# Earlier adding of bank halves in four FFNs, and another order of the first pairs in a fifth

## The chip, the core and the metric

The program runs on one core of one Trainium2 chip. The time is device microseconds of one execution; the kernel before took 1358.48 us (median of three runs, 1358.3 to 1360.25). The engines are named as in the profile: PE (TensorE, matmuls), PEld (its weight loads), DVE (VectorE), ACT (ScalarE), POOL (GpSimd) and SP, whose queue issues the weight transfers.

## What is computed

256 tokens of width 1024 pass through a first block of two layers and a second block of one. In every layer of the first block stands a pair of gated FFNs around a mixer; the second block ends in one FFN with a short convolution. Everything is float32.

```python
# block 1, twice: FFN, mixer, FFN
h = rms_norm(x, ffn1_norm[layer])
x = x + 0.5 * (silu(h @ w_gate) * (h @ w_up)) @ w_down      # 1024 -> 2816 -> 1024
h = rms_norm(x, mix_norm[layer]);  x = x + mixer(h)          # even_mixer, then odd_mixer
h = rms_norm(x, ffn2_norm[layer]); x = x + 0.5 * swiglu(h)   # a second FFN
# block 2
x = layer_norm(x); x = layer_norm(ALPHA * x + mixer2(x) @ w_o)
h = causal_conv3(x @ w_up)                                   # 1024 -> 2 * 2816
a, u = split(h);   x = layer_norm(ALPHA * x + (gelu(a) * u) @ w_down)
```

## The kernel before

Activations lie transposed: the 1024 features are 8 tiles of 128 partitions, each with 256 tokens in its free dimension. All weights stand in one stream of blocks of 128x1024 floats, in the order of their use. SP loads a block into `raw` (5 buffers), ACT casts it to float32r as `wh` (line 314), DVE takes the rest, `wl = raw - wh` (line 316); each of these has 5 buffers, so up to five blocks are ready ahead of PE. A product of one weight tile with the 8 input tiles (`proj_t`) uses one block and leaves its result in one PSUM bank.

In the FFNs of block 1 the moving operand is both parts of the input side by side, `xh | xl`, 512 columns (`mm2`, lines 334, 335 and 337). So a bank holds two halves of 256 tokens that still have to be added: `fold` (lines 597 to 600) copies the right half with ACT and adds the left one with DVE. The bank is free after that. Six banks take turns (`six_ps`: four named mm, two named sc); the others, aux, serve small products.

The function `ffn` (lines 549 to 595) goes over 22 tiles of the hidden layer. Each is a pair of products, gate and up. For a pair it issues both products, adds the gate's halves into `s`, multiplies by `rb` (the token factor of the norm, 1/rms of each token on all partitions), takes Silu with ACT into `sg`, adds the up product's halves into `hp`, multiplies, and splits the result into its high and low part `h`. `rb` comes from `norm_bcast` (lines 528 to 540): a product with ones for the sum of squares (line 532), three ACT steps and three DVE steps. In the first FFN the squares themselves are taken by ACT in between (`norm_sum_first`).

Block 2 starts its projections before its layer norm is known: the first six products are made of the raw input (`def_proj`, line 1090) and corrected afterwards on DVE (`def_out`, lines 1108 and 1110) into tiles `dv`. This happens ahead of its mixer (`mix2`) and again ahead of its FFN. Between them `ln_apply` makes the normed input tiles `xs` (lines 1059 to 1063).

The function `ffn2` (line 1463) goes over 22 pairs as well. The first six results, three pairs, are those `dv` tiles; from pair 3 on it issues the products. Each result gets its convolution: one ACT step (line 1478) and two DVE steps that add the shifted tokens (1479 and 1481), which for a product also free its bank. ACT takes Gelu (1484), POOL multiplies (1486), ACT and DVE split (1487 and 1488).

Tiles of 256 columns come from one set of 14 buffers (`tmp`, tag c1), those of 512 from one of 7 (c2). The tile framework's planner sets the order on each engine: it goes by the order in which the code is written and by when its own plan has an instruction ready. On the chip each engine then runs its list in order.

```python
s = self.tmp("s", T)
self.fold(s, pg)
nc.vector.tensor_tensor(out=s, in0=s, in1=self.rb, op=ALU.mult)
```

Of the kernel before, what the change touches and what calls it, by code (L numbers as in the profile page):

```python
# [9 lines left out]
F32 = mybir.dt.float32  # L10
F32R = mybir.dt.float32r
AF = mybir.ActivationFunctionType
ALU = mybir.AluOpType
AX = mybir.AxisListType

P = 128
T = 256
# [3 lines left out]
KF = DFF // P  # L21
BLK = 1024
NSLOT = 22
LOOK = 6
NWB = 5
NRAW = 5
NC1 = 14
NC2 = 7
WARM = 18
NDEF = 6  # L30
# [181 lines left out]
class K:  # L212
# [21 lines left out]
    def tmp(self, tag, n, bufs=2, dt=F32):  # L234
        if n == T:
            return self.tp.tile([P, T], dt, tag="c1", name=tag, bufs=NC1)
        if n == 2 * T:
# [290 lines left out]
    def norm_bcast(self):  # L528

        nc = self.nc  # L530
        ps = self.aux_ps()[:, :T]
        nc.tensor.matmul(ps, self.ones, self.acc, start=True, stop=True)
        u, y, t = [self.tmp(f"nb{i}", T) for i in range(3)]
        nc.scalar.activation(u, ps, AF.Identity, scale=1.0 / D, bias=self.eps[:, 0:1])
        nc.scalar.activation(y, u, AF.Ln)
        nc.scalar.activation(y, y, AF.Exp, scale=-0.5)
        nc.vector.scalar_tensor_tensor(out=t, in0=y, scalar=-0.5, in1=y, op0=ALU.mult, op1=ALU.mult)
        nc.vector.tensor_tensor(out=t, in0=t, in1=u, op=ALU.mult)
        self.rb = self.tmp("rb", T)
        nc.vector.scalar_tensor_tensor(out=self.rb, in0=t, scalar=1.5, in1=y, op0=ALU.add, op1=ALU.mult)  # L540

    def ln_exp_tables(self):
# [5 lines left out]
    def ffn(self, next_gain, first=False):  # L548
        nc = self.nc
        h2 = [self.slot(f"h{i}", F32R) for i in range(KF // 2)]  # L550
        if not first:
            self.norm_bcast()
        for i in range(KF):
            pg = self.six_ps()
            if i == 0 and first:
                self.look = 2
                self.proj_t(pg)
                self.norm_sum_first()
                self.norm_bcast()
                self.look = LOOK  # L560
            else:
                self.proj_t(pg)
            pu = self.six_ps()
            self.proj_t(pu)
            s = self.tmp("s", T)
            self.fold(s, pg)
            nc.vector.tensor_tensor(out=s, in0=s, in1=self.rb, op=ALU.mult)
            sg = self.tmp("sg", T)
            self.last_act = nc.scalar.activation(sg, s, AF.Silu)
            hp = self.tmp("hp", T)  # L570
            self.fold(hp, pu)
            nc.vector.tensor_tensor(out=hp, in0=hp, in1=sg, op=ALU.mult)
            nc.scalar.activation(self.hi(h2, i), hp, AF.Copy)
            nc.vector.tensor_tensor(out=self.lo(h2, i), in0=hp, in1=self.hi(h2, i).bitcast(F32), op=ALU.subtract)
        self.ln_exp_tables()
        if next_gain is not None:
            self.norm_begin()
        n = 0
        for j in range(KD):
            ps = self.mm_ps()  # L580
            for k in range(KF):
                if n % 8 == 0:
                    wh, wl = self.block()
                s = slice((n % 8) * P, (n % 8 + 1) * P)
                n += 1
                self.mm2(ps, wh[:, s], wl[:, s], self.both(h2, k), k == 0, k == KF - 1)
            t = self.tmp("t", T)
            self.fold(t, ps)
            nc.vector.scalar_tensor_tensor(out=t, in0=t, scalar=0.5, in1=self.rb,
                                           op0=ALU.mult, op1=ALU.mult)  # L590
            nc.vector.tensor_tensor(out=self.x(j), in0=self.x(j), in1=t, op=ALU.add)  # L591
            if next_gain is not None:
                self.norm_tile(j, next_gain)
            else:
                self.trans_tile(j)
# [504 lines left out]
    def def_out(self, i):  # L1100

        nc = self.nc
        ps = self.dps.pop(i)
        wb = self.tmp("wgb", 2, 4)
        nc.vector.tensor_copy(wb, ps[:, 256:258])
        v = self.tmp("dv", T)
        r = self.mA[nc.vector]
        nc.vector.scalar_tensor_tensor(out=v, in0=self.mA[nc.gpsimd][:, :T], scalar=wb[:, 0:1], in1=ps[:, :T],
                                       op0=ALU.mult, op1=ALU.subtract)
        nc.vector.tensor_tensor(out=v, in0=v, in1=r[:, T:], op=ALU.mult)  # L1110
        return v, wb[:, 1:2]
# [351 lines left out]
    def ffn2(self, first):  # L1463
        nc = self.nc
        h2 = [self.slot(f"h{i}", F32R) for i in range(KF // 2)]
        x2 = [self.slot(f"x2n{i}") for i in range(2)]
        for i in range(KF):
            y = []
            for u in range(2):
                c = u * KF + i  # L1470
                t = self.tmp("s" if u == 0 else "sg", T)
                if 2 * i + u < len(first):
                    ps, b = first[2 * i + u]
                    nc.scalar.activation(ps, ps, AF.Identity, bias=b)
                else:
                    ps = self.six_ps()[:, :T]
                    self.proj_t(ps)
                nc.scalar.activation(t, ps, AF.Identity, scale=self.col("conv2", c), bias=self.col("convb", c))
                nc.vector.scalar_tensor_tensor(out=t[:, 1:], in0=ps[:, :T - 1], scalar=self.col("conv1", c),
                                               in1=t[:, 1:], op0=ALU.mult, op1=ALU.add)  # L1480
                nc.vector.scalar_tensor_tensor(out=t[:, 2:], in0=ps[:, :T - 2], scalar=self.col("conv0", c),  # L1481
                                               in1=t[:, 2:], op0=ALU.mult, op1=ALU.add)
                y.append(t)
            self.last_act = nc.scalar.activation(y[0], y[0], AF.Gelu)
            hp = self.tmp("hp", T)
            nc.gpsimd.tensor_tensor(out=hp, in0=y[0], in1=y[1], op=ALU.mult)
            nc.scalar.activation(self.hi(h2, i), hp, AF.Copy)
            nc.vector.tensor_tensor(out=self.lo(h2, i), in0=hp, in1=self.hi(h2, i).bitcast(F32), op=ALU.subtract)
            if 8 <= i < 16:
                j = i - 8  # L1490
                ps = self.aux_ps()
                for tt in range(2):
                    nc.tensor.transpose(ps[:, tt * P:(tt + 1) * P], self.x(j)[:, tt * P:(tt + 1) * P], self.ident)
                    nc.scalar.activation(x2[tt][:, j * P:(j + 1) * P], ps[:, tt * P:(tt + 1) * P], AF.Copy,
                                         scale=2.0 ** 0.25)
        self.ln_exp_tables()
        gb = [self.slot(n) for n in ("lng", "lnb")]
        for t, n in zip(gb, ("f2g", "f2b")):
            nc.gpsimd.dma_start(out=t, in_=self.aps[n].to_broadcast([P, D]))
        st = self.tmp("bst", 36, 1).rearrange("p (t h s) -> p t h s", t=2, h=3)  # L1500
        n = 0
        for gi, (c0, cw) in enumerate(((0, 512), (512, 256), (768, 256))):
            ps = [self.mm_ps()[:, :cw] for _ in range(2)]
            held = []
            for k in range(KF):
                o = n % BLK
                if o == 0:
                    wh, wl = self.block()
                n += cw
                w = wh[:, o:o + cw], wl[:, o:o + cw]  # L1510
                late = gi == 2 and k >= KF - 16
                if late:
                    held.append((k, w))
                for tt in range(1 if late else 2):
                    self.down(ps[tt], h2, k, tt, w)
            for tt in range(2):
                if tt:
                    for k, w in held:
                        self.down(ps[1], h2, k, 1, w)
                x = x2[tt][:, c0:c0 + cw]  # L1520
                nc.vector.tensor_tensor(out=x, in0=ps[tt], in1=x, op=ALU.add)
                nc.vector.bn_stats(out=st[:, tt, gi], in_=x)
                if gi == 2:
                    self.ffn2_out(tt, x2[tt], st[:, tt], gb)
# [112 lines left out]
```

## Time and profile before

| | |
|---|---|
| median of 3 runs | 1358.48 us (1358.3 to 1360.25) |
| profiled execution, its own time | 1355.37 us |
| its span, first to last instruction | 1353.6 us |
| PE / PEld busy | 1315.9 us (97%) / 1165.5 us (86%) |
| DVE / ACT / POOL busy | 996.2 us (74%) / 812.5 us (60%) / 218.9 us (16%) |
| weight transfers | 231.49 MB, 48.5% of 16 DMA engines |
| mean granted TensorE clock | 0.997 |

The page's busy times are sums over stages; where PE stops is read from the waits and the timeline. In a timeline row stand the start and the duration in us, the engine, the line, the operation, the tiles written and read, and in brackets the idle time of the engine ahead of it with what ended it. The end of a matmul is modelled and overlaps the next one, so the pace of PE is read from start to start.

### The profile page before, as it was taken

What the parts mean: (1) busy time and instruction counts of PE and PEld (TensorE: products, weight loads), DVE (VectorE), ACT (ScalarE), POOL (GpSimd) and SP (SyncE); (2) the same over time, 40 slices, a digit from 0 to 9 for tenths busy, and PEclk for the clock granted to TensorE, in tenths of its full rate; (3) what the DMA queues carried; (4) which work ended last, traced back from release to release, by engine and by line L of the source; (5) the groups of instructions that cost most, each with busy time, mean ns of one, the idle gap of its engine ahead of it and who ended that gap; (6) DMA issues with size and microseconds to landing.
All of it is one profiled execution on the core that took longest, in us unless ns stands there. A gap on an engine that the chain in (4) does not pass through costs nothing.

```text
span 1353.6 us, 22502 instructions
## 1 busy us (share of the span) xinstructions
PE 1315.9 (97%) x8250; PEld 1165.5 (86%) x8250; DVE 996.2 (74%) x1860; ACT 812.5 (60%) x1491; POOL 218.9 (16%) x260
## 2 busy tenths in 40 slices
PE   8999999899999999999999999999999999889997
PEld 7888887798888888888899888888877888889987
DVE  7877677668776768776658777777877768887754
ACT  7655545756555446555468746555577556866642
POOL 2000141021000210001334340000134022321101
PEclk9999999999999999999999999999999999999999
DMA  8555565025555555555565345555555304355561
GB/s 291 187 187 188 188 203 185 1 98 198 187 188 187 189 184 188 187 187 186 187 233 187 126 145 190 190 190 187 187 187 179 117 32 156 119 193 174 196 208 46
DMA packets 64367, 231.49 MB, mean 171 GB/s; under 512 B 7352, under 2 KB 7488, under 8 KB 64256
## 3 DMA queue, kind: packets, MB, share of 16 engines
q1 hardware_dynamic: 61632, 221.41, 48.5%
q0 software_dynamic: 2480, 8.63, 1.8%
q8 instruction: 65, 1.06, 0.3%
q14 instruction: 46, 0.38, 0.1%
q10 hardware_dynamic: 144, 0.00, 0.0%
HBM read 228.96 MB, written 1.06 MB: 170 GB/s over the span
## 4 chain that ended last, share of the span: by engine, by line
PE 88%; DVE 5%; ACT 4%; issue 2%; DMA 0%; POOL 0%; SPq 0%; DVEq 0%; ACTq 0%
PE mm L337 25%; PE mm L335 14%; PE sc L337 7%; PE mm L341 5%; PE mm L342 5%; PE mm L343 5%; PE sc L335 4%; PE mm L372 4%; PE mm L370 4%; PE mm L371 4%; PE mm L334 3%; DVE wl L316 1%; PE sc L334 1%; PE mm L664 1%; ACT wh L314 1%
## 5 line engine op out<-in xcount | busy, mean ns | idle before, releaser
L316 DVE TENSOR_TENSOR wl<-raw,wh 128x1024 fp32r<-128x1024 f32 x409 | 507.0, 1242 | 250.3 <-ACT wh L314 249.0
L314 ACT ACTIVATE wh<-raw 128x1024 fp32r<-128x1024 f32 x417 | 440.2, 1059 | 416.1 <-issue 200.5
L337 PE MATMUL mm<-xs,wh 128*128 128x512 f32 x826 | 294.5, 396 | 0.0
L335 PE MATMUL mm<-xs,wl 128*128 128x256 f32 x944 | 244.1, 279 | 1.8 <-DVE wl L299 1.0
L337 PE MATMUL mm<-h,wh 128*128 128x512 f32 x672 | 237.9, 398 | 0.0
L335 PE MATMUL mm<-h,wl 128*128 128x256 f32 x704 | 191.5, 280 | 0.0
L335 PEld LDWEIGHTS mm<-xs,wl 128*128 128x128 f32 x944 | 177.7, 188 | 12.8 <-DVE wl L299 1.6
L337 PEld LDWEIGHTS mm<-xs,wh 128*128 128x128 f32 x826 | 154.6, 188 | 31.7 <-DVE xs L444 0.3
L337 PEld LDWEIGHTS mm<-h,wh 128*128 128x128 f32 x672 | 126.0, 188 | 29.2
L337 PE MATMUL sc<-xs,wh 128*128 128x512 f32 x406 | 144.8, 396 | 0.0
L335 PEld LDWEIGHTS mm<-h,wl 128*128 128x128 f32 x704 | 132.9, 189 | 3.1
L470 POOL TENSOR_TENSOR sq<-xt 128x256 f32<-128x256 f32 x40 | 34.8, 872 | 547.1 <-DVE xt L591 342.5
L335 PE MATMUL sc<-xs,wl 128*128 128x256 f32 x464 | 120.2, 280 | 0.0
L341 PE MATMUL mm<-xs,wh 128*128 128x256 f32 x384 | 109.9, 289 | 5.3 <-DVE s L1481 4.7
L342 PE MATMUL mm<-xs,wh 128*128 128x256 f32 x384 | 109.5, 286 | 1.1 <-DVE xs L1063 1.1
L343 PE MATMUL mm<-xs,wl 128*128 128x256 f32 x384 | 109.3, 286 | 0.0
L335 PEld LDWEIGHTS sc<-xs,wl 128*128 128x128 f32 x464 | 87.5, 189 | 5.1
L337 PEld LDWEIGHTS sc<-xs,wh 128*128 128x128 f32 x406 | 76.1, 188 | 15.5
L341 PEld LDWEIGHTS mm<-xs,wh 128*128 128x128 f32 x384 | 73.7, 193 | 7.4 <-issue 6.4
L342 PEld LDWEIGHTS mm<-xs,wh 128*128 128x128 f32 x384 | 74.2, 193 | 1.5 <-DVE xs L1063 1.3
L343 PEld LDWEIGHTS mm<-xs,wl 128*128 128x128 f32 x384 | 74.1, 193 | 0.9 <-issue 0.8
L372 PE MATMUL mm<-wh,xs 128*128 128x512 f32 x144 | 56.1, 394 | 1.2 <-DVE xs L1063 1.2
(392 smaller groups left out, 2573.8 us busy)
## 6 DMA issues: line engine op xcount, KB each, us to landing
raw<-wst SPq DMA_DIRECT2D x417, 512.0 KB, 3.3
m1b<-m1bias POOLq DMA_DIRECT2D x8, 512.0 KB, 5.1
xt<-xT SPq DMA_DIRECT2D x4, 256.0 KB, 5.0
patf<-m2pat POOLq DMA_DIRECT2D x2, 512.0 KB, 7.9
kb<-scr POOLq DMA_DIRECT2D x2, 512.0 KB, 3.9
out<-x2n SPq DMA_DIRECT2D x4, 256.0 KB, 2.0
raw<-wst SPq DMA_DIRECT2D x2, 256.0 KB, 4.6
m0tab<-m0tab POOLq DMA_DIRECT2D x1, 512.0 KB, 5.2
```

The lines of the kernel that those rows point to most:

```text
L314: self.nc.scalar.activation(wh[:, c], r[:, c], AF.Copy)
L316: e.tensor_tensor(out=wl[:, c], in0=r[:, c], in1=wh[:, c].bitcast(F32), op=ALU.subtract)
L334: mm(ps, wh, x2, start=True, stop=False)
L335: mm(ps[:, :T], wl, x2[:, :T], start=False, stop=False, skip_group_check=True)
L337: mm(ps, wh, x2, start=False, stop=last)
L341: mm(ps, wh, xh, start=first, stop=False)
L342: mm(ps, wh, xl, start=False, stop=False)
L343: mm(ps, wl, xh, start=False, stop=last)
L370: mm(ps, xh, wh, start=first, stop=False)
L371: mm(ps, xh, wl, start=False, stop=False)
L372: mm(ps, xl, wh, start=False, stop=last)
L470: nc.gpsimd.tensor_tensor(out=sq, in0=self.x(j), in1=self.x(j), op=ALU.mult)
```

## The change

Three things are edited. In `ffn` each product's halves are added right behind that product, ahead of the token factor, Silu writes over `s`, and in the first FFN the squares and the norm come after the first add. The token factor and its helpers get tiles of their own (nb with 3 buffers, rb with 2), c1 shrinks to 11, and `dv` tiles are taken as halves of 512-column tiles of c2. In `ffn2` the pairs are worked in the order 3, 4, 0, 5, 6, 1, 7, 8, 2, and then 9 to 21: the three pairs that come from `dv` stand later.

```diff
-NC1 = 14
+NC1 = 11
@@ norm_bcast
-        u, y, t = [self.tmp(f"nb{i}", T) for i in range(3)]
+        u, y, t = [self.tp.tile([P, T], F32, tag="nb", name=f"nb{i}", bufs=3) for i in range(3)]
...
-        self.rb = self.tmp("rb", T)
+        self.rb = self.tp.tile([P, T], F32, tag="rb", name="rb", bufs=2)
@@ ffn
-            pg = self.six_ps()
-            if i == 0 and first:
-                self.look = 2
-                self.proj_t(pg)
-                self.norm_sum_first()
-                self.norm_bcast()
-                self.look = LOOK
-            else:
-                self.proj_t(pg)
-            pu = self.six_ps()
-            self.proj_t(pu)
-            s = self.tmp("s", T)
-            self.fold(s, pg)
+            y = []
+            for u in range(2):
+                ps = self.six_ps()
+                if i + u == 0 and first:
+                    self.look = 2
+                self.proj_t(ps)
+                t = self.tmp("s" if u == 0 else "hp", T)
+                self.fold(t, ps)
+                if i + u == 0 and first:
+                    self.norm_sum_first()
+                    self.norm_bcast()
+                    self.look = LOOK
+                y.append(t)
+            s, hp = y
             nc.vector.tensor_tensor(out=s, in0=s, in1=self.rb, op=ALU.mult)
-            sg = self.tmp("sg", T)
-            self.last_act = nc.scalar.activation(sg, s, AF.Silu)
-            hp = self.tmp("hp", T)
-            self.fold(hp, pu)
-            nc.vector.tensor_tensor(out=hp, in0=hp, in1=sg, op=ALU.mult)
+            self.last_act = nc.scalar.activation(s, s, AF.Silu)
+            nc.vector.tensor_tensor(out=hp, in0=hp, in1=s, op=ALU.mult)
@@ def_out
-        v = self.tmp("dv", T)
+        if i % 2 == 0:
+            self.dv = self.tmp("dv", 2 * T)
+        v = self.dv[:, i % 2 * T:(i % 2 + 1) * T]
@@ ffn2
-        for i in range(KF):
+        for i in (3, 4, 0, 5, 6, 1, 7, 8, 2, *range(9, KF)):
```

How the lists change is seen at two places. The numbers of lines behind the edit are smaller by two in the changed kernel up to `def_out` (600 becomes 598, 1063 becomes 1061) and the same again in `ffn2`.

DVE at the start of the first FFN, before: L537, 538 and 540 make the token factor, L600 is the add of two halves, L567 the product with the factor.

```order
L1123 TENSOR_SCALAR g_9973<-g_9973 128x8
L316 TENSOR_TENSOR wl<-raw,wh 128x1024 x3
L537 SCALAR_TENSOR_TENSOR nb_221<-nb_220 128x256
L715 TENSOR_SCALAR nsink<-m0row 128x8
L538 TENSOR_TENSOR nb_221<-nb_221,nb_219 128x256
L316 TENSOR_TENSOR wl<-raw,wh 128x1024
L540 SCALAR_TENSOR_TENSOR rb<-nb_221,nb_220 128x256
L600 TENSOR_TENSOR s<-mm,s 128x256
L567 TENSOR_TENSOR s<-s,rb 128x256
L316 TENSOR_TENSOR wl<-raw,wh 128x1024
L600 TENSOR_TENSOR hp<-mm,hp 128x256
```

The same place in the changed kernel, where L598 is the add; one more, of the first product, stands 16 rows further up:

```order
L1123 TENSOR_SCALAR g_9885<-g_9885 128x8
L598 TENSOR_TENSOR hp<-mm,hp 128x256
L598 TENSOR_TENSOR s<-mm,s 128x256
L598 TENSOR_TENSOR hp<-mm,hp 128x256
L316 TENSOR_TENSOR wl<-raw,wh 128x1024
L598 TENSOR_TENSOR s<-sc,s 128x256
L316 TENSOR_TENSOR wl<-raw,wh 128x1024
L598 TENSOR_TENSOR hp<-sc,hp 128x256
L537 SCALAR_TENSOR_TENSOR nb_224<-nb_223 128x256
L713 TENSOR_SCALAR nsink<-m0row 128x8
L538 TENSOR_TENSOR nb_224<-nb_224,nb_222 128x256
L540 SCALAR_TENSOR_TENSOR rb<-nb_224,nb_223 128x256
```

All six banks are emptied ahead of the token factor in the changed list; before, none was.

DVE where `ffn2` begins, before: the convolution steps of the dv pairs stand between the last `xs` tiles, and those of the first product (s<-mm) behind all of them.

```order
L1063 TENSOR_TENSOR xs_12396<-xt,xs_12396 128x256
L1479 SCALAR_TENSOR_TENSOR s<-dv,cols,s 128x255
L1479 SCALAR_TENSOR_TENSOR sg<-dv,cols,sg 128x255
L1481 SCALAR_TENSOR_TENSOR s<-dv,cols,s 128x254
L1488 TENSOR_TENSOR h_12681<-hp,h_12681 128x256
L1481 SCALAR_TENSOR_TENSOR sg<-dv,cols,sg 128x254
...
L316 TENSOR_TENSOR wl<-raw,wh 128x1024 x2
L1488 TENSOR_TENSOR h_12681<-hp,h_12681 128x256
L316 TENSOR_TENSOR wl<-raw,wh 128x1024 x3
L1479 SCALAR_TENSOR_TENSOR s<-mm,cols,s 128x255
```

In the changed kernel (L1061 is the step of line 1063 before):

```order
L1061 TENSOR_TENSOR xs_12305<-xt,xs_12305 128x256 x2
L316 TENSOR_TENSOR wl<-raw,wh 128x1024
L1479 SCALAR_TENSOR_TENSOR s<-mm,cols,s 128x255
...
L1481 SCALAR_TENSOR_TENSOR s<-mm,cols,s 128x254
L1479 SCALAR_TENSOR_TENSOR sg<-mm,cols,sg 128x255
...
L1481 SCALAR_TENSOR_TENSOR sg<-mm,cols,sg 128x254
L316 TENSOR_TENSOR wl<-raw,wh 128x1024 x2
...
L1488 TENSOR_TENSOR h_12588<-hp,h_12588 128x256
...
L1479 SCALAR_TENSOR_TENSOR s<-dv,cols,s 128x255
L1479 SCALAR_TENSOR_TENSOR sg<-dv,cols,sg 128x255
...
L1479 SCALAR_TENSOR_TENSOR s<-sc,cols,s 128x255
```

The banks of the first products are worked right behind the last `xs` tiles; the first dv pair stands behind four of them.

## Rows read from the trace of the kernel before

**Rows 1.** The page: busy times, and the chain that ended last by engine.

```profile
PE 1315.9 (97%) x8250; PEld 1165.5 (86%) x8250; DVE 996.2 (74%) x1860; ACT 812.5 (60%) x1491; POOL 218.9 (16%) x260
...
PE 88%; DVE 5%; ACT 4%; issue 2%; DMA 0%; POOL 0%; SPq 0%; DVEq 0%; ACTq 0%
```

**Rows 2.** Waits of PE: tile, line, releaser; us in total, times, longest.

```profile
PE mm L341 <- DVE s L1481: 4.7, 1, 4.7
PE mm L874 <- ACT pT L657: 2.8, 2, 2.0
...
PE mm L334 <- DVE hp L600: 1.4, 3, 0.7
...
PE mm L372 <- DVE xs L1063: 1.2, 1, 1.2
PE mm L342 <- DVE xs L1063: 1.1, 1, 1.1
...
PE mm L334 <- DVE s L600: 0.7, 2, 0.4
...
PE sc L334 <- DVE s L600: 0.4, 1, 0.4
PE sc L334 <- DVE hp L600: 0.3, 1, 0.3
```

**Rows 3.** Timeline of PE at the start of the first FFN.

```profile
24.14 0.39 PE L337 MATMUL sc<-xs,wh 128*128 128x512 f32 x1
...
24.61 0.40 PE L335 MATMUL sc<-xs,wl 128*128 128x256 f32 x2
...
26.93 0.40 PE L337 MATMUL sc<-xs,wh 128*128 128x512 f32 x1
27.70 0.47 PE L334 MATMUL mm<-xs,wh 128*128 128x512 f32 x1 [0.38 <-DVE s L600]
28.01 0.40 PE L335 MATMUL mm<-xs,wl 128*128 128x256 f32 x2
```

**Rows 4.** Timeline of DVE in the same stretch.

```profile
26.81 0.42 DVE L540 SCALAR_TENSOR_TENSOR rb<-nb,nb 128x256 f32<-128x256 f32 x1
27.14 0.42 DVE L600 TENSOR_TENSOR s<-mm,s 128x256 f32<-128x256 f32 x1
...
30.45 0.42 DVE L600 TENSOR_TENSOR hp<-mm,hp 128x256 f32<-128x256 f32 x1 [0.78 <-ACT hp L599]
```

**Rows 5.** Windows: length, busy us of PE, PEld, DVE, ACT, POOL; clock; DMA.

```profile
240.00:243.00 3.00, 2.63 (x21) 2.30 (x21) 2.76 (x7) 2.34 (x7) 0.00 (x0) 1.00 0.00 0
...
1183.20:1188.00 4.80, 0.09 (x2) 0.04 (x1) 4.80 (x8) 2.09 (x5) 2.58 (x1) 1.00 0.82 289
1188.00:1191.60 3.60, 3.60 (x18) 3.60 (x19) 2.72 (x7) 3.00 (x7) 1.30 (x2) 0.56 0.81 328
...
1195.00:1215.00 20.00, 20.00 (x169) 20.00 (x169) 16.08 (x26) 13.81 (x26) 2.65 (x4) 1.00 0.55 185
```

**Rows 6.** Timeline of PE where ffn2 begins.

```profile
1187.99 0.36 PE L341 MATMUL mm<-xs,wh 128*128 128x256 f32 x1 [4.71 <-DVE s L1481]
...
1188.41 0.41 PE L341 MATMUL mm<-xs,wh 128*128 128x256 f32 x1
...
1191.61 0.38 PE L341 MATMUL mm<-xs,wh 128*128 128x256 f32 x1
```

**Rows 7.** Timeline of DVE in the same stretch.

```profile
1170.42 0.47 DVE L1479 SCALAR_TENSOR_TENSOR s<-dv,cols,s 128x255 f32<-128x255 f32 x1
...
1178.72 0.47 DVE L1481 SCALAR_TENSOR_TENSOR sg<-dv,cols,sg 128x254 f32<-128x254 f32 x1
...
1181.72 3.48 DVE L316 TENSOR_TENSOR wl<-raw,wh 128x1024 fp32r<-128x1024 f32 x3
...
1187.37 0.47 DVE L1481 SCALAR_TENSOR_TENSOR s<-mm,cols,s 128x254 f32<-128x254 f32 x1
```

**Rows 8.** Timeline of POOL in the same stretch.

```profile
1182.08 3.70 POOL L1486 TENSOR_TENSOR hp<-s,sg 128x256 f32<-128x256 f32 x1 [4.36 <-ACT s L1484]
```

## The prediction

> **What bounds the kernel now.** I read the page first, then the waits of PE, then the timeline of PE and DVE around the longest of them. PE is busy for 97% of the span and holds 88% of the chain that ended last; DVE, the next, is busy for 74% and holds 5% [rows 1]. The reader is to see that only time in which PE waits, or runs slowly, can be won or lost: the change adds and removes no matmul and no weight transfer, and one operation of DVE or ACT more or less costs nothing while PE has a bank to write and a block of weights to read.
>
> The list of PE's waits then says where such time is [rows 2]. One wait is far longer than the others, 4.7 us, and its releaser is line 1481 of `ffn2`, a DVE step that empties a bank. Four groups have the adds of `ffn`, line 600, as releaser: 1.4, 0.7, 0.4 and 0.3 us, together 2.8 us in 7 waits. Two have the low part of the normed input, line 1063: 1.2 and 1.1 us, one at each of the two places where `ln_apply` runs. Those three sorts of waits are what the edits can reach.
>
> **The adds right behind each product.** PE fills six banks while the token factor is being made. In the first FFN DVE writes `rb` at 26.81 and only then adds the first two halves, at 27.14 [rows 4]; PE has ended its sixth product and sits until 27.70 [rows 3]. The next bank comes from the up product's add at 30.45, which waited for ACT [rows 4], and PE waits again. The change's list on DVE has the adds of all six banks ahead of the factor, none of which needs it. So both waits lose their cause.
>
> What one costs is more than the idle time. Undisturbed, the step from a product's last matmul over the first of the next one to its second takes 24.61 - 24.14 = 0.47 us; across the wait it takes 28.01 - 26.93 = 1.08 us, 0.61 more, of which 0.38 is shown as idle [rows 3]. With the same 0.23 beside each of the seven waits the sum is 2.8 + 7 x 0.23 = 4.4 us. The opposite bound: the same adds must still be done, and if PE waited as long for weights that DVE prepares later, nothing would be won, 0 us; if the adds also kept the factor's chain from starting, a wait could grow by the length of a bank's add, 0.42 us [rows 4], seven times, 2.9 us lost. I take the whole 4.4: the adds use DVE time in which it otherwise waits, they hold up at most a few `wl` of which five blocks are kept ahead, and a late factor only delays Silu and the tiles `h`, which PE first reads in the down product after all 22 pairs. What is late next in this stretch is the factor itself, with up to four pairs of sums waiting in buffers for it; DVE then does their products in a row, and PE has empty banks meanwhile.
>
> Silu in place over `s`, tiles of their own for the factor, and c1 with 11 buffers cost nothing: with one tile fewer in each pair the smaller set holds five pairs of sums, and a pair lasts longer on PE than the whole chain of the factor. The list of the first FFN has the squares behind the first add and two more casts of weights, so that the sum over ones comes later, in the seventh product instead of the fifth; PE does not wait for its result.
>
> **The pairs of `ffn2`.** Before, DVE works the three dv pairs from 1170.42 to 1178.72 and beyond, then five blocks' `wl`, of which three stand at 1181.72 for 3.48 us, and reaches the last step of the first product's bank at 1187.37 [rows 7]. PE had filled the banks of pairs 3, 4 and 5, and its next matmul starts at 1187.99 after 4.71 us [rows 6]. While it sits the DVE is fully busy, 4.80 of 4.80 us, so it is the order of DVE's work that makes PE wait [rows 5]. In the change's list the steps of that first product stand right behind the last `xs` tiles, ahead of every dv pair.
>
> To the 4.71 us comes what the wait does to PE's clock. In the window behind it the granted clock is 0.56, the lower level of 1.2 GHz for most of it, where 1.00 is 2.4 GHz [rows 5]. From 1188.41 to 1191.61 run 15 matmuls, 0.213 us each [rows 6]; at full clock 169 of them take 20 us, 0.118 each [rows 5]. That is 15 x 0.095 = 1.4 us lost. The restart from 1187.99 to 1188.41, 0.42 us, is three steps, 0.35 at pace [rows 6]; with 0.2 us for it and for refilling the pipeline, an estimate, the wait costs 6.3 us.
>
> Not all of this need come back. DVE has the same work in another order. At pace it is busy 16.08 us of 20, in which PE makes 169 / 24 = 7 products [rows 5]; so it has 0.56 us to spare for each product. Three dv pairs of five steps of 0.47 us [rows 7] are 7.1 us, which needs some 13 products to catch up. Six banks are a reserve of 6 x 24 x 0.118 = 17 us, and the change puts one dv pair after every two others, 2.35 us at a time, with `wl` between. The fifth bank, behind the first dv pair, is the tight one: I expect PE to wait for it, or for a block, between 0 us and one dv pair, 2.35 us, and take 0.8 us. Then 5.5 us are won here; the bounds are 6.3 and, if as long a wait comes back, 0.
>
> Here a rule of the notes bears. After waits of up to 2.0 us, the longest one for the transposed weights of attention [rows 2], the clock in the next 3 us stands at 1.00 [rows 5]. The Trainium skill ("TensorE: Matmul & The Clock Gate", HAM oscillation) says that waits between groups of matmuls let the gate fall, so that each next group starts cold. The trace shows it for the 4.7 us wait and not for one of 2.0; by the rule a rest of 2 us would cost 3.4 instead of 2.0, by the row 2.0, and the sum here goes by the row.
>
> **The input tiles.** The new lists put the first steps of line 1063 ahead of work that stood before them, by about two DVE steps of 0.4 us, at both `ln_apply` places. The two waits are 2.3 us together [rows 2]. I take 0.8 us; the bounds are 2.3 won and, since the same shuffle could put another tile later, 1.0 lost. The `dv` tiles in c2 and the moved steps also change the lists inside the mixer of block 2 a little; I take 0, within 1.5 us either way, somewhat more than either wait of line 1063.
>
> **The sum.** 4.4 + 5.5 + 0.8 = 10.7 us. Against the profiled execution, 1355.37 us with a span of 1353.6, it gives 1344.7. The median of the runs is 3.1 us above that execution; from it, 1358.48 - 10.7 = **1347.8 us**.
>
> **Rivals.**
>
> 1. *The dv pairs hold a bank up through POOL.* POOL's product took 3.70 us at 1182.08 [rows 8], where DVE made three `wl` at the same time [rows 7]; ACT's next split waits for it, and behind that split stand its casts and convolution steps. The Trainium skill ("SBUF — State Buffer", Who interferes with whom) says that a DVE instruction with two inputs in SBUF contends with what GpSimd reads; these rows agree. With dv pairs spread among the `wl`, it could meet three more times. If a bank comes late by 3.7 us once, and the 1.4 of the clock stays, 5.1 of the 6.3 return: 1358.48 - 4.4 - 1.2 - 0.8 = 1352.1. Against it: PE has a reserve of several products.
> 2. *The FFN starts give nothing.* ACT must copy the half of a bank for each add, and its copies now stand between the casts of weights; if PE then waits for a block instead of a bank, the 4.4 us stay: 1352.2. For it: DVE's second add waited for ACT [rows 4]. Against it: ACT is busy for 60% only [rows 1].
> 3. *The stall moves.* The planner's order is good only in its plan, and waits of the same kind come up elsewhere: in the mixer of block 2 and behind the first three pairs. With 2.9 us lost at the FFN starts instead of 4.4 won, and 5.5 won in `ffn2`, minus 1.0 at the input tiles and 1.5 in the mixer, it is 1358.4: no change.
> 4. *Slower: each dv pair makes the stall again.* The place is the start of `ffn2`. If DVE's five steps of a dv pair always stand ahead of what PE needs next, and DVE has no slack there, the wait of 6.3 us comes three times, 12.6 more than now; with the 4.4 and 0.8 of the other places that is 1358.48 + 12.6 - 5.2 = 1365.9. It decides from the point where a dv pair and the `wl` beside it take longer than the products in the six banks, 17 us; the rows give 2.35 us for the pair, so it is unlikely.
>
> **How the numbers follow.** The forecast has 0.58, the rivals in order 0.17, 0.12, 0.08 and 0.05. A measurement of this kernel can tell 0.2%, 2.7 us, from no change. Faster by more: the forecast and the first two, 0.87, and a small part of the third, 0.01; within it: most of the third, 0.07; slower: 0.05. The range goes from 1343.0 (4.4 + 6.3 + 2.3 + 1.5 = 14.5, with 1 us for the runs' spread) to 1354.0, which takes in the first two rivals with 1.8 us above them.
>
> **What would show it.** In the changed profile: no wait for the adds of line 598 in the four FFN starts; no wait over 2.5 us for line 1481, and a clock of 1.00 in the stretch where it was 0.56; DVE's convolution step of the first product about 10 us earlier against the last `xs` tile; PE busy the same 1316 us less 1 to 2. Wrong it would be if waits for `wl` or `wh` appear in the FFN starts, if the half clock stays in `ffn2`, or if the mixer of block 2 has grown by more than 2 us.

## The result and the profile after

The changed kernel took 1343.49 us (median of 4 runs, 1342.89 to 1344.84) against 1358.48: 15.0 us less, a ratio of 0.9893 [0.9879, 0.9907]. A second set of five runs gave 1344.65 beside 1358.08 for the kernel before, 0.9909 [0.9894, 0.9924], so 13.4 us. The profiled execution took 1342.89 us with a span of 1341.1, which is 12.5 less than that of before. One execution of the first experiment's kernel took 4567 us, with its matmuls about 3.6 times as far apart and the casts of DVE and ACT about as long as ever; its ratio goes without it.

The page of the changed kernel answers [rows 1]: the busy times, and the chain that ended last by engine.

```profile
PE 1314.3 (98%) x8250; PEld 1168.2 (87%) x8250; DVE 999.4 (75%) x1860; ACT 811.5 (61%) x1491; POOL 218.0 (16%) x260
...
PE 92%; DVE 3%; ACT 2%; issue 1%; DMA 0%; SPq 0%; POOL 0%; DVEq 0%; ACTq 0%
```

PE's work is the same, DVE's share of the chain fell from 5% to 3% and ACT's from 4% to 2%. The waits of PE say which ones went [rows 2]:

```profile
PE mm L872 <- ACT pT L655: 2.8, 2, 2.0
PE mm L342 <- DVE xs L1061: 2.1, 1, 2.1
...
PE mm L372 <- DVE xs L1061: 0.4, 1, 0.4
```

No row is left for the adds (line 598 now) nor for line 1481. Of the two waits for the input tiles one is shorter (1.2 to 0.4 us), the other longer (1.1 to 2.1).

DVE in the first FFN [rows 4]: the adds now stand ahead of the factor.

```profile
24.32 0.41 DVE L598 TENSOR_TENSOR s<-mm,s 128x256 f32<-128x256 f32 x1
24.65 0.41 DVE L598 TENSOR_TENSOR hp<-mm,hp 128x256 f32<-128x256 f32 x1
...
28.71 0.42 DVE L598 TENSOR_TENSOR hp<-sc,hp 128x256 f32<-128x256 f32 x1
...
30.02 0.43 DVE L540 SCALAR_TENSOR_TENSOR rb<-nb,nb 128x256 f32<-128x256 f32 x1
```

The factor itself came 3.2 us later than before (30.02 against 26.81), and PE did not wait for it. PE went from the sixth bank to the next one at pace, without the 0.38 us of [rows 3]:

```profile
26.05 0.40 PE L337 MATMUL sc<-xs,wh 128*128 128x512 f32 x1
26.28 0.39 PE L334 MATMUL mm<-xs,wh 128*128 128x512 f32 x1
26.74 0.39 PE L337 MATMUL mm<-xs,wh 128*128 128x512 f32 x1
```

DVE at the start of `ffn2` [rows 7]:

```profile
1169.39 1.22 DVE L316 TENSOR_TENSOR wl<-raw,wh 128x1024 fp32r<-128x1024 f32 x1 [4.37 <-ACT wh L314]
1170.53 0.48 DVE L1479 SCALAR_TENSOR_TENSOR s<-mm,cols,s 128x255 f32<-128x255 f32 x1
...
1172.06 0.47 DVE L1481 SCALAR_TENSOR_TENSOR s<-mm,cols,s 128x254 f32<-128x254 f32 x1
...
1182.24 0.48 DVE L1479 SCALAR_TENSOR_TENSOR s<-dv,cols,s 128x255 f32<-128x255 f32 x1
```

The first bank is done at 1172.06 + 0.47, before at 1187.37 + 0.47. DVE even sat idle for 4.4 us ahead of it, until ACT had cast the next block; why ACT came so late with that cast the profile doesn't show. The windows over the same place [rows 5]: the wait for `xs`, the 3 us behind it, and the stretch in which PE had stood before.

```profile
1156.00:1158.60 2.60, 0.39 (x1) 0.19 (x1) 2.60 (x7) 2.60 (x6) 0.00 (x0) 1.00 0.76 233
1158.70:1161.70 3.00, 3.00 (x15) 3.00 (x16) 3.00 (x7) 2.83 (x7) 0.00 (x0) 0.56 0.48 145
1182.00:1192.00 10.00, 10.00 (x86) 10.00 (x85) 9.70 (x20) 8.51 (x17) 4.41 (x3) 1.00 0.55 190
```

The half clock has moved: it now stands behind the 2.1 us wait for `xs`.

How far the changed kernel is ahead is read from the start of the same matmul in both traces, every eighth of the 7,356 matmuls with streamed weights; behind each place stands the lead there and what that stretch gave:

| stretch, time in the trace of before | lead at its end, us | gained, us |
|---|---|---|
| up to 22.8 (start) | 0.70 | 0.70 |
| to 31.0 (first FFN) | 1.50 | 0.80 |
| to 816.1 (three more FFN starts: 1.2, 1.1, 1.2) | 5.15 | 3.65 |
| to 1036.8 (first `ln_apply`, start of block 2's mixer) | 7.29 | 2.14 |
| to 1160.2 (rest of the mixer) | 6.89 | -0.40 |
| to 1172.1 (second `ln_apply`) | 5.61 | -1.28 |
| to 1192.4 (start of `ffn2`) | 12.49 | 6.88 |
| to the end | 12.37 | -0.12 |

The 0.70 of the first row is hardly the change's: a second trace of the same kernel has 0.24 there, and those of the experiments lie between 2.2 us behind before and 0.5 ahead.

### The profile page after: what moved, and what is told of

Read it like the earlier page. It is cut to its first block, busy times and chain, and to the rows that moved or that the text cites. A ratio compares the mean times of both kernels' runs of the same rounds, so it can differ in the third digit from the quotient of the medians.

```text
span 1341.1 us, 22591 instructions
## 1 busy us (share of the span) xinstructions
PE 1314.3 (98%) x8250; PEld 1168.2 (87%) x8250; DVE 999.4 (75%) x1860; ACT 811.5 (61%) x1491; POOL 218.0 (16%) x260
## 4 chain that ended last, share of the span: by engine, by line
PE 92%; DVE 3%; ACT 2%; issue 1%; DMA 0%; SPq 0%; POOL 0%; DVEq 0%; ACTq 0%
PE mm L337 26%; PE mm L335 14%; PE sc L337 7%; PE mm L341 5%; PE mm L342 5%; PE mm L343 5%; PE sc L335 4%; PE mm L372 4%; PE mm L370 4%; PE mm L371 4%; PE mm L334 3%; PE sc L334 1%; DVE wl L316 1%; PE sc L343 1%; PE sc L342 1%
```

## The experiments

**The adds without the factor's own tiles.** The new body of `ffn` in the kernel before; `nb` and `rb` stay in c1, and dv tiles and pairs are as before.

```diff
-            pu = self.six_ps()
-            self.proj_t(pu)
-            s = self.tmp("s", T)
-            self.fold(s, pg)
+                t = self.tmp("s" if u == 0 else "hp", T)
+                self.fold(t, ps)
```

> The kernel before with the new body of ffn alone (adds right behind each product, Silu in place, norm of the first FFN behind its first add); the token factor keeps its tiles in the common set c1 of 14, the pairs of ffn2 keep their order. Theory (the code order of the adds wins the FFN starts): the seven waits for line 598 go, 4.4 us less than before, and the 4.7 us wait for line 1481 stays. Rival (the order alone does not free the banks, the factor's own tiles do, since in this kernel's list for DVE five of the first six adds stand behind the factor): the first FFN keeps a wait of 0.3 to 1 us for the adds, 0 to 2 us less than before in all, possibly slower.

It took 1361.44 us, 1.0022 [1.0010, 1.0034] of before: 3 us slower. For its trace the same kernel ran once more:

> The new body of ffn on the common set c1 of 14 once more, for its profile. Theory (the banks wait for the factor, since its tiles come from the same set as the sums and the list has five of six adds behind it): in the first FFN a wait of PE of 0.5 to 3 us for line 598, and waits for it in the other three FFN starts too, at least 2.8 us in all; the wait for the first convolution step of ffn2 stays. Rival (the 3 us lost lie elsewhere, in attention or ahead of ffn2): the FFN starts are free of waits.

1361.4 us. DVE in its first FFN, and four of PE's waits:

```profile
30.45 0.42 DVE L540 SCALAR_TENSOR_TENSOR rb<-nb,nb 128x256 f32<-128x256 f32 x1
...
32.46 0.42 DVE L598 TENSOR_TENSOR hp<-mm,hp 128x256 f32<-128x256 f32 x1
...
34.12 0.41 DVE L598 TENSOR_TENSOR s<-mm,s 128x256 f32<-128x256 f32 x1
```

```profile
PE mm L341 <- DVE s L1479: 5.7, 1, 5.7
...
PE mm L334 <- DVE hp L598: 2.8, 1, 2.8
...
PE mm L334 <- DVE s L598: 0.4, 1, 0.4
...
PE sc L334 <- DVE s L598: 0.3, 1, 0.3
```

Five of the first six adds still stand behind the factor, which the later norm also puts off, and PE waits 2.8 us for the up product's add. (Line 1479 is 1481 of before.) The order of the code alone moves nothing forward there. At the three later FFN starts it does: one short wait each is left at two of them, none at the third, and the lead over before grows by 0.6, 0.6 and 0.95 us, where the changed kernel gains 1.2, 1.1 and 1.2. The first FFN loses 2.2, so the four starts together come out at nothing. What makes the kernel slower lies elsewhere in its trace: 2.7 us in attention at a lower clock, of which more below, 1.1 behind 1036.8, again at a lower clock (0.79 up to 1045), and 2.2 where `ffn2` begins. How much of that the edit causes these runs do not tell.

**The factor's own tiles alone, and with the adds.**

```diff
-NC1 = 14
+NC1 = 11
-        self.rb = self.tmp("rb", T)
+        self.rb = self.tp.tile([P, T], F32, tag="rb", name="rb", bufs=2)
```

> The kernel before with the factor's own tiles and c1 of 11 alone; the body of ffn, the dv tiles and the order of pairs as before. Theory (own tiles alone do nothing where the code adds the up half behind Silu): one add of six ahead of the factor, the FFN starts win 0 to 0.5 us of 2.8, the time within 2 us of before. Rival (they are the whole gain there): 3 to 5 us less.

1358.66 us, 1.0006 [0.9993, 1.0020]: no change. Its waits at the FFN starts, three of 0.9 us for the up product's add and one more of 0.9 in a sc bank, were each longer than those of before, but four instead of seven, and the lead at the four starts stays within 0.1 us:

```profile
PE mm L334 <- DVE hp L600: 2.7, 3, 0.9
```

> The kernel before with the new body of ffn and the factor's own tiles (c1 11), without the dv tiles in c2 and without the new order of pairs. Theory (adds and own tiles together free the banks): no wait for line 598, 4.4 us less than before, with the 4.7 us stall of ffn2 there, perhaps longer by 1 us with six dv tiles in a c1 of 11. Rival (without the dv tiles moved out, c1 of 11 is too small in the mixer and ffn2): 2 us or more of new waits behind 1000 us, no gain.

1352.10 us, 0.9951 [0.9938, 0.9964], 5.9 us less. No wait for an add is left, and at the end of the fourth FFN start its trace leads that of before by 4.8 us, of which 0.25 from the start; the four starts give 0.8, 1.2, 1.1 and 1.2, as in the changed kernel. The stall of `ffn2` is there:

```profile
PE mm L341 <- DVE s L1479: 4.9, 1, 4.9
```

So the own tiles alone do nothing, and the adds alone lose at the first FFN start what they gain at the other three; together they give all four. The own tiles came with the smaller c1 in both runs; own tiles beside a c1 of 14 were not tried.

**The pairs and dv tiles alone.** The kernel before with the last two parts of the change's diff.

> The kernel before with the new order of pairs in ffn2 and the dv tiles as halves of c2, nothing else. Theory (the stall and its half clock are the ffn2 share): 6.3 to 6.5 us less than before, the waits of 0.3 to 0.7 us at the FFN starts unchanged, together 2.8 us. Rival (part of the gain behind 1150 us comes from the freed tiles of c1 or the planner's other shuffles): less than 5 or more than 8 us.

1348.13 us, 0.9925 [0.9912, 0.9938]: 10.2 us less, in the rival's range. By its trace it is 7.5, and the rest comes from the base, of which more below. Two of PE's waits:

```profile
PE mm L342 <- DVE xs L1063: 2.1, 1, 2.1
...
PE mm L334 <- DVE hp L600: 1.4, 3, 0.7
```

The stall is gone and the adds' waits are the same as before. From 1169 to 1215 us its trace gains 7.0 us on that of before, and 2.0 between 1000 and 1053, at the first `ln_apply` and the start of the mixer; the run with adds and own tiles, which has the dv tiles in c1, gains nothing there, and the next one, with dv tiles in c2 and the old order of pairs, gains them too. So the 2 us come with the dv tiles in c2, and so does the longer wait for `xs`, which the run with adds and own tiles hasn't either.

**The natural order of pairs in the changed kernel.**

```diff
-        for i in (3, 4, 0, 5, 6, 1, 7, 8, 2, *range(9, KF)):
+        for i in range(KF):
```

> The changed kernel with the pairs of ffn2 in the order 0, 1, 2, ... again. Theory: the wait of PE for line 1481 and the half clock behind it come back, 6.3 us over the changed kernel; FFN starts without waits, 4.4 us and some 1 to 2 of shuffle below the kernel before. Rival (the dv tiles in c2 alone remove most of the stall, since they free six tiles of c1): within 2 us of the changed kernel.

1351.75 us, 0.9948 [0.9935, 0.9961] of before and 7.1 to 8.3 us over the changed kernel's two medians. The wait for line 1481 is back:

```profile
PE mm L341 <- DVE s L1481: 5.3, 1, 5.3
```

So the dv tiles in c2 do not remove the stall, the order does; the order without them was not tried.

**Three dv pairs in a row, early and late.** The order 3, 4, 5, 0, 1, 2, 6 and on:

> The changed kernel with the pairs of ffn2 as 3, 4, 5, 0, 1, 2, 6, ...: the three dv pairs still behind three others, but one after the other. Theory (what made the stall is that dv steps stood ahead of the first banks; once six banks are emptied first, 7.1 us of dv steps fit into the 17 us that PE needs for six banks): within 1.5 us of the changed kernel, waits of PE at line 1481 under 1 us. Rival (DVE has no slack there and needs the dv pairs spread among others): a wait of 2 to 5 us for line 1481 or for a block of weights comes back, 3 to 7 us over the changed kernel.

1351.04 us, 6.4 over the changed kernel in the same set: the rival. DVE, where the first two dv pairs begin and where the next bank is done, and the matmul of PE that waited for it:

```profile
1186.24 0.96 DVE L1479 SCALAR_TENSOR_TENSOR s<-dv,cols,s 128x255 f32<-128x255 f32 x1
...
1189.78 0.95 DVE L1479 SCALAR_TENSOR_TENSOR s<-dv,cols,s 128x255 f32<-128x255 f32 x1
...
1199.47 0.47 DVE L1481 SCALAR_TENSOR_TENSOR s<-mm,cols,s 128x254 f32<-128x254 f32 x1
```

```profile
1200.09 0.55 PE L341 MATMUL mm<-xs,wh 128*128 128x256 f32 x1 [4.52 <-DVE s L1481]
```

PE ran out of free banks at 1195.57. At 1186.24 it therefore had 9.3 us of free banks left, not the 17 of six empty ones, and DVE needed 13.7 us to its next bank: three dv pairs, the `wl` of three blocks between them and one behind, and the split parts. 13.7 - 9.3 = 4.4; that is the wait of 4.5 taken apart, not a second measurement of it.

The same row of three, behind six others:

> The changed kernel with the pairs of ffn2 as 3 to 8, 0, 1, 2, 9, ...: the three dv pairs in a row as in the run that lost 6.4 us, but three pairs later. Theory (DVE is busy for 10.0 of 10 us there, so it builds no reserve by being later; three dv pairs in a row take 10.6 us of it with a block's low part each, and it is the row that makes PE wait): a wait of 3 to 5 us behind the third one, 5 to 7 us over the changed kernel. Rival (three products later DVE has caught up): a wait under 1.5 us, within 2 us of the changed kernel.

1345.30 us against 1344.65: no loss, and here I was wrong. The windows are the stretch of the early row's start, the one ahead of the late row, and the late row:

```profile
1185.00:1195.00 10.00, 10.00 (x85) 10.00 (x85) 9.61 (x18) 7.48 (x15) 3.03 (x2) 1.00 0.59 202
1195.00:1203.00 8.00, 8.00 (x69) 8.00 (x68) 6.38 (x11) 5.98 (x11) 1.49 (x2) 1.00 0.58 197
1203.00:1213.50 10.50, 10.50 (x90) 10.50 (x90) 10.50 (x20) 9.44 (x21) 4.51 (x3) 1.00 0.46 151
```

In the 10 us in which the early row had stood DVE has hardly any pause; after that it is busy for 6.38 of 8.00 us: it has caught up, and PE is busy through the whole row. So how late the dv pairs come counts as much as how they are spread.

**The input tiles earlier, with three orders of pairs.**

```diff
-                    if i in (1, 3):
-                        self.ln_apply(g, b, range(4) if i == 1 else range(4, 8))
+                    if i in (0, 1):
+                        self.ln_apply(g, b, range(4) if i == 0 else range(4, 8))
```

> The changed kernel with ln_apply behind the first and the second def_out instead of the second and the fourth. In the changed kernel PE waits 2.1 us for the first low part of xs ahead of ffn2, and the granted clock of the 3 us behind is 0.56. Theory (def_out and two casts of weights ahead of the first xs make it late): the wait falls below 1 us, the clock stays at 1.00, 2 to 4 us less than the changed kernel. Rival (ACT, which makes the high parts of xs, sets the time, or a bank of a later deferred product comes late instead): within 1 us of the changed kernel, or slower with a new wait for a bank.

1345.83 us: not below the changed kernel. Its waits show the exchange:

```profile
PE sc L341 <- DVE s L1481: 1.9, 1, 1.9
...
PE mm L342 <- DVE xs L1061: 0.4, 1, 0.4
```

The wait for `xs` shrank and PE came 3 us earlier, but DVE did not, it was even 2.5 us later at the first bank of `ffn2`: behind the first dv pair PE ran out of banks. (The expectations below call this a wait for a block; the waits put it down to the bank.)

> The inputs earlier as in the kernel with ln_apply behind the first and second def_out, and the pairs of ffn2 as 0, 3, 4, 5, 1, 6, 7, 8, 2, ...: one dv pair where DVE sat idle for 4.4 us ahead of the first banks of ffn2 in the changed kernel. Theory (DVE idles there, so a dv pair is free, and DVE has more in reserve when the later ones come): the 1.9 us wait for a block at 1190 us is gone, the 2.1 us wait for xs too, 2 to 4 us less than the changed kernel. Rival (its steps stand among the last xs in DVE's list and make those late): a wait for xs of 1 to 2 us comes back, no gain.

1345.09 us, no gain: the wait for the bank was 1.2 us, and one of 0.7 for a block's `wl` came up.

> The inputs earlier as above, and the pairs of ffn2 as 3, 4, 5, 6, 0, 7, 8, 9, 1, 10, 11, 12, 2, ...: every dv pair behind one pair more. Theory (DVE gains 0.56 us on PE with each product at pace, so later dv pairs meet a fuller reserve): the 1.9 us wait for a block at 1190 us is gone, 2 to 4 us less than the changed kernel. Rival (DVE's reserve is set by the banks and the five blocks, not by how late the pair comes; the wait only moves): a wait of 1 us or more at another dv pair, within 1 us of the changed kernel.

1341.83 us, 0.9885 [0.9866, 0.9904] of before. Its runs, 1340.54 to 1342.79, lie below all five of the changed kernel in the same set, 1343.19 to 1346.31: the fastest version here. Its waits, and the 3 us behind the wait for `xs`:

```profile
PE mm L341 <- DVE s L1481: 0.4, 1, 0.4
PE mm L342 <- DVE xs L1061: 0.4, 1, 0.4
```

```profile
1157.40:1160.40 3.00, 2.95 (x22) 2.71 (x23) 3.00 (x7) 3.00 (x5) 0.00 (x0) 1.00 0.64 213
```

The clock stays up, where 15 matmuls ran in 3 us it is 22 now.

**The changed kernel once more.**

> The changed kernel once more, beside the kernels of this set. Theory (the kernel before loses 2 to 3 us in most runs to a lower clock in attention that its profiled execution did not have, so 15.0 us between the medians is 12.5 of the change's own and 2.5 of that): a median of 1343 to 1346, and in its own profile a clock below 1.00 between 235 and 295 us wherever it lies 2 us or more over 1342.9. Rival (the whole 15 us are the change's): a median of 1343.5 and no relation to that clock.

1344.65 us; its profiled execution took 1346.20. Its trace is 3.3 us behind the first one of the same kernel, 0.5 of it from the start and 2.8 between 230 and 292 us, in attention. Three windows there, of the changed kernel's first profile, of its second, and of the kernel before:

```profile
235.00:245.00 10.00, 7.79 (x39) 6.71 (x40) 7.96 (x22) 8.39 (x28) 0.86 (x4) 0.83 0.00 0
245.00:255.00 10.00, 8.75 (x72) 8.09 (x71) 6.79 (x27) 8.29 (x26) 0.00 (x0) 1.00 0.01 2
285.00:295.00 10.00, 9.48 (x76) 9.00 (x77) 5.00 (x11) 4.17 (x9) 2.28 (x3) 1.00 0.00 1
```

```profile
235.00:245.00 10.00, 7.80 (x39) 6.40 (x38) 8.11 (x23) 8.38 (x28) 0.87 (x4) 0.78 0.02 9
245.00:255.00 10.00, 8.78 (x59) 7.75 (x58) 5.94 (x23) 7.18 (x22) 0.00 (x0) 0.88 0.01 2
285.00:295.00 10.00, 9.14 (x62) 8.53 (x61) 2.90 (x6) 1.68 (x5) 0.00 (x0) 0.83 0.05 17
```

```profile
235.00:245.00 10.00, 7.79 (x48) 6.35 (x46) 8.53 (x28) 7.70 (x25) 0.86 (x4) 1.00 0.14 50
245.00:255.00 10.00, 7.48 (x57) 6.36 (x56) 6.79 (x26) 8.53 (x27) 0.00 (x0) 1.00 0.01 2
285.00:295.00 10.00, 9.14 (x73) 8.52 (x73) 4.13 (x10) 2.66 (x7) 0.74 (x2) 1.00 0.03 12
```

The seventh number is the granted clock. In the profiled execution of before it stood at 1.00 in all three.

## Why the prediction was right, and where it was not

**The forecast and its sum.** The time lies in the range, 4.3 us below the forecast and only half a us above the range's lower end. The highest terms together made 14.5 and the medians differ by 15.0, so without the 1 us for the spread of the runs it would lie outside: that part was luck. By the traces the terms of the sum are worth 4.45 + 6.88 + 0.46 = 11.8 us, against 10.7; the other 3 us come from the base.

**The adds.** 4.4 us were forecast; the four FFN starts gave 0.80 + 3.65 = 4.45. Idle time plus 0.23 us of refilling beside each wait was the right price. The step that failed beside it is the sentence that puts tiles of their own for the factor among what costs nothing, as if they were an accessory, and gives the 4.4 us to the adds: without those tiles the four starts come out at nothing, and the tiles alone are worth nothing. I had seen the list of the whole change only, and had not asked which edit put the adds there. Why the planner puts five adds behind the factor when all share c1 is not shown by a run; that the sums then have to take their turn behind the factor's tiles in one set of buffers is argued. So is that it takes the tiles and not the smaller c1 that came with them.

**The pairs of `ffn2`.** Forecast 5.5, which is 6.3 less a residue of 0.8; measured 6.9 in the changed kernel and 7.0 with the pairs and dv tiles alone. The stall itself, with clock and restart, was 6.4 (12.49 less the lead of 6.07 at 1182.2); the rest came in small steps before it. No residue came: at the fifth bank nothing waited. The half clock was priced rightly, and its window is at 1.00 now.

But the reserve was mis-sized. Six banks of 17 us would hold only if DVE had emptied all of them when a dv pair begins. The early row of three shows 9.3 us, and a dv pair with its block costs DVE 3.5 us (1186.24 to 1189.78), not 2.35. The slower rival named the right place and mechanism; its reserve should have been 9.3 us and not 17, and what kept the change from it is that two pairs stand between the dv pairs.

**The input tiles.** Forecast 0.8 in all. Measured 2.14 up to 1036.8, where about 1.2 are the input tiles and 1.15 the start of the mixer, and then -0.40 and -1.28: about 0.5 together. The sign differed by place. At the second one two casts of weights and `def_out` steps stand ahead of the first `xs`, and the clock went down behind the wait, which no term of mine held.

**The rule that I set aside.** After a 2.0 us wait in attention the clock stood at 1.00 in the one trace that I had [rows 5], and I went by that row. The changed kernel shows the other outcome: behind 2.1 us in front of `ffn2` the clock is 0.56, and in attention, behind waits of the same length, it was 0.83 and 0.78 over 10 us. The Trainium skill ("TensorE: Matmul & The Clock Gate", HAM oscillation) tells of a kernel in which waits between groups of matmuls let each next group start cold; its waits are longer than these, and the prediction left that out. The rows show that the clock can fall behind 2 us and does not each time, so one execution at 1.00 did not settle it.

**The base of the sum.** I put the difference between the profiled execution and the median, 3.1 us, down to nothing in particular. The runs of before in the experiments' sets spread from 1354.8 to 1362.4, and for 45 of them the mean granted clock is on record. The eleven fastest, up to 1355.4 us, have 0.996 or 0.997, as the profiled execution had; the others, from 1356.2 on, have 0.995 or less, those at 1358 to 1358.5 us 0.992 or 0.993. The changed kernel's first four runs have 0.996 or 0.997. So the median of before, 1358.48, is by its time one of the runs at a lower clock, and it was set beside runs at the higher one. At 0.996 and 0.997 alone the median is 1355.2 us for before and 1343.4 for the changed kernel (five runs in two sets): 11.8 us less, and some 3 of the 15.0 are this spread. Where the clock was lower only traces can tell: eight of the twelve others (the one at 4567 us aside) lost 1.2 to 3.1 us in attention, 160 to 312 us, against that of before, and four lost nothing.

**POOL.** The first rival did not come: POOL's products took 0.7 to 1.8 us in this stretch, never 3.7. The contention that it named is there with the roles exchanged:

```profile
1190.61 1.82 POOL L1486 TENSOR_TENSOR hp<-s,sg 128x256 f32<-128x256 f32 x1 [1.22 <-ACT s L1484]
```

```profile
1191.74 0.97 DVE L1479 SCALAR_TENSOR_TENSOR s<-dv,cols,s 128x255 f32<-128x255 f32 x1
```

A dv step of DVE that overlapped POOL's product took 0.97 us instead of 0.47, while POOL's took 1.82 instead of 0.74. The Trainium skill ("SBUF — State Buffer", Who interferes with whom) says that DVE with two inputs in SBUF and a reading GpSimd contend; the trace agrees, at 0.5 us for two of the three dv pairs.

## What to carry to other kernels

When the engine that empties the banks lags behind PE, work that frees no bank belongs behind the point where it has caught up, and the reserve at that point is counted from the banks that are empty then, not from all there are. When buffers come from one shared set, moving an instruction ahead in the code need not move it ahead in the engine's list (why is argued here, not shown), so a change of order and one of tiles must be tried together and apart. A gain in front of such a stretch is kept only if the lagging engine gains as well: the inputs made earlier were worth nothing until the dv pairs moved back by one.

## What the runs showed of the hardware

The granted clock behind a wait of about 2 us is not the same in each execution of one kernel: the changed kernel's attention ran 2.8 us longer in one profile than in the other with waits of the same length, and nothing in the program differed. A difference of 0.2% between two profiles of this kernel is of that size; it takes several runs set beside each other at the same mean granted clock, or a comparison stage by stage, to tell it from a change.
